# The last pair's products ahead of the first inverse's, in a mixed trunk of gating, RWKV-7 and gated FFN layers

## The chip, the cores and the metric

One Trainium2 chip, one core. The metric is the device time of one execution in microseconds (us). The kernel before takes 1244.08 us, the median of 3 runs (1243.03 to 1244.97). For a measurement of this kernel, 0.2% (2.5 us) is about what can be told from no change.

Engines: TensorE (PE, with PEld for its weight loads), VectorE (DVE), ScalarE (ACT), GpSimd (POOL) and SyncE (SP, which here issues DMAs). L12 is line 12 of the kernel.

## The reference, cut to what matters

Two residual layers on x of 512 positions by 1024 channels, float32: a gMLP layer and an RWKV-7 layer, each followed by a convolutional FFN. The change lies in the RWKV-7 layer:

```python
r = xr @ w_r;  k = xk @ w_k;  v = xv @ w_v
w = -softplus(-(w0 + tanh(xw @ w1) @ w2)) - 0.5
a = sigmoid(a0 + (xa @ a1) @ a2)
g = sigmoid(xg @ g1) @ g2
kk = l2norm_per_head(k * k_k)
k = k * (1 + (a - 1) * k_a)
# per head (16 heads of 64), S is 64 x 64:
#   S_t = S_{t-1} diag(exp(-exp(w_t))) + (S_{t-1} (-kk_t)) (kk_t a_t)^T + v_t k_t^T;  y_t = S_t r_t
y = group_norm(y) * ln_w + ln_b
bonus = sum_per_head(r * k * r_k) * v
out = ((y + bonus) * g) @ w_o
```

The recurrence is not run position by position. The 512 positions are cut into 8 chunks of 64, and in each chunk the steps' influence on each other is solved by the inverse of a 64 x 64 triangular matrix, for every chunk and head.

## The kernel before, in words

Activations lie with channels on the 128 partitions and the 512 positions along the free axis. A weight product is done in three passes on pieces of float32 (high times high, high times low, low times high: L325 to L327), 128 x 128 weights against 512 positions.

The RWKV-7 layer (`rwkv_main`) works on 8 *pairs* of heads (128 channels each), in two groups g of four. Its parts are Python generators, and each `yield` is a step by which they are woven together:

- `pairs` (the main line at first): for pair p the decays (`decay`), the scaled operands (`operands`, all on VectorE but a few copies), and the products (`products`): L973 for each half of the chunks into banks "aux" and "us", the masks L977 on VectorE, three DMAs of the result each (L981), then L988 into `bt` (L991) and its DMA (L992). Three steps a pair; the third one only goes on with the decays of a later pair.
- `invert(g)`: the inverses of a group's chunks. It copies blocks (L1046), transposes them on VectorE (`turn`, L1051), runs 30 dependent steps of elimination on VectorE (L1069, L1070; a yield after every second one), transposes twice more, and then does eight batches of small products on TensorE (L1090, L1093), with ScalarE's copies L1098, L1103 and L1105 between. For g = 1 a `turn` is four instructions of 256 columns, for g = 0 one of 1024. Its steps are 1 (after the first transpose), 15 (elimination), 1 (after the last transpose) and 8 (batches); for g = 1 one more at the start.
- `fill`: work for TensorE that is put between the steps of the others. It is the chain of `projections` (key and value weights; a value takes four steps of six matmuls, 512 positions each), `gates` (the gate's low-rank products, 17 steps) and `project` (the output projection, 12 steps for g = 0, then g = 1). A value m (`value`) is copied into `v` (L854), centred (L868, ScalarE's four copies L873), and then its bonus product L883 is multiplied by v on VectorE (L885) into `rt`, and ScalarE adds the bias ln_b there (L886).
- `scan(g)`: 8 chunks of three steps. L1301 are the chunk's first products; they are copied to `wt` (L1304); L1314 multiplies by the inverse; L1321 and L1326 are the state and the output. `finish` normalizes two chunks' outputs (squares L1342, sums L1347, a power on POOL, L1357, transposes L1363, L1366).

In `gates`, two steps issue idle matmuls (`idle`, L1124: two products into a spare place), and the step behind them issues one more such pair each time it is asked before the first group's last normalization has been traced (`while 0 not in normed`). Then `gate` multiplies `rt` by the gate (L1209) and splits it for the projection.

The order is written out at the end of `rwkv_main`. `weave(main, side, fill, rate, lag, side_rate)` runs main step by step; after every step `rate` fills are due, and `side_rate` steps of the side line. The stages are: pairs 0 to 3 with fill; pairs 4 to 7's first step, with `invert(0)` at the side; the last pair's other two steps; what is left of `invert(0)` in a loop; scan 0 with `invert(1)` at the side; scan 1; and a hand-written end. `tc.issue_after(x)` puts instructions behind x on its engine. From the program's order and a cost model of its own the framework's scheduler fixes the order of each engine's instructions ahead of the run.

PSUM has four tags of two banks each: "mm" for the projections, "aux", "e" and "us".

## Time and profile before

| what | value |
|---|---|
| median of 3 runs | 1244.08 us (1243.03 to 1244.97) |
| the profiled execution | 1245.55 us, its span 1243.7 us |
| granted TensorE clock, mean | 0.996 |
| TensorE busy | 1226.8 us (99%) |
| VectorE, ScalarE, POOL busy | 851.1, 633.1, 81.4 us |
| pairs 4 to 7 and the first inverse | about 649 to 726 us of the span |
| scan 0, scan 1 | about 726 to 784, 784 to 840 us |

The span goes from the first to the last instruction. A row of a group gives line, engine, operation, out<-in, shape and count, then busy time in us and the mean in ns of one, then the idle time of the engine just before and what ended it. A timeline row begins with start and length in us; [2.28 <-DVE rt L885] says that the engine had been idle for 2.28 us and that this instruction released it. A row on one line of the code gives the least, median and greatest ns of one, and first and last start. Under it stand who waited for whom, in us and times.

### The profile page before, as it was taken

What the parts mean: (1) busy time and instruction counts of PE and PEld (TensorE: products, weight loads), DVE (VectorE), ACT (ScalarE), POOL (GpSimd) and SP (SyncE); (2) the same over time, 40 slices, a digit from 0 to 9 for tenths busy, and PEclk for the clock granted to TensorE, in tenths of its full rate; (3) what the DMA queues carried; (4) which work ended last, traced back from release to release, by engine and by line L of the source; (5) the groups of instructions that cost most, each with busy time, mean ns of one, the idle gap of its engine ahead of it and who ended that gap; (6) DMA issues with size and microseconds to landing.
All of it is one profiled execution on the core that took longest, in us unless ns stands there. A gap on an engine that the chain in (4) does not pass through costs nothing.

```text
span 1243.7 us, 19411 instructions
## 1 busy us (share of the span) xinstructions
PE 1226.8 (99%) x7535; PEld 1000.2 (80%) x7535; DVE 851.1 (68%) x1418; ACT 633.1 (51%) x1089; POOL 81.4 (7%) x106
## 2 busy tenths in 40 slices
PE   9999999999999999999999999999999999999997
PEld 6878888888888888877887777778888888888886
DVE  5566578888876454675899698776777777872323
ACT  6544455555554343466787667424544444543232
POOL 1100200000000001000000013222000000000000
PEclk9999999999999999999999899999999999999999
DMA  7232457887556776326888797654223223333332
GB/s 273 94 105 82 132 180 246 246 249 241 192 172 193 220 226 196 109 81 182 220 242 237 188 280 233 219 171 135 85 102 102 90 97 102 97 88 104 97 93 81
DMA packets 125133, 201.65 MB, mean 162 GB/s; under 512 B 39857, under 2 KB 63153, under 8 KB 125041
## 3 DMA queue, kind: packets, MB, share of 16 engines
q10 hardware_dynamic: 38976, 112.87, 29.5%
q1 hardware_dynamic: 86064, 87.54, 22.6%
q8 instruction: 59, 0.97, 0.3%
q14 instruction: 34, 0.27, 0.1%
HBM read 152.93 MB, written 47.45 MB: 161 GB/s over the span
## 4 chain that ended last, share of the span: by engine, by line
PE 91%; DVE 4%; DMA 3%; ACT 1%; issue 0%; SPq 0%; POOL 0%; DVEq 0%; POOLq 0%; ACTq 0%
PE mm L325 9%; PE mm L327 9%; PE mm L326 9%; PE aux L325 6%; PE aux L326 6%; PE aux L327 6%; PE e L325 6%; PE e L326 6%; PE us L325 6%; PE e L327 6%; PE us L327 6%; PE us L326 6%; PE us L1314 1%; PE aux L973 1%; PE aux L988 1%; PE us L1321 1%
## 5 line engine op out<-in xcount | busy, mean ns | idle before, releaser
L237 ACT CAST w<-w 128x512 fp32r<-128x512 f32 x340 | 206.5, 611 | 359.8 <-PE aux L327 92.6
L238 DVE TENSOR_TENSOR w<-w,w 128x512 fp32r<-128x512 f32 x340 | 230.5, 680 | 180.2 <-ACT w L237 179.6
L325 PE MATMUL mm<-mxh,w 128*128 128x512 f32 x408 | 167.9, 412 | 2.7 <-DVE rt L885 2.6
L327 PE MATMUL mm<-mxh,w 128*128 128x512 f32 x408 | 161.1, 395 | 0.0
L326 PE MATMUL mm<-mxl,w 128*128 128x512 f32 x408 | 160.6, 394 | 0.0
L325 PEld LDWEIGHTS mm<-mxh,w 128*128 128x128 f32 x408 | 77.0, 189 | 22.8 <-DVE rt L885 3.3
L327 PEld LDWEIGHTS mm<-mxh,w 128*128 128x128 f32 x408 | 77.0, 189 | 17.1 <-issue 0.8
L326 PEld LDWEIGHTS mm<-mxl,w 128*128 128x128 f32 x408 | 77.1, 189 | 16.2 <-issue 1.7
L575 ACT ACTIVATE cv<-z,par 128x512 f32<-128x512 f32 x88 | 71.7, 817 | 26.5 <-DVE z L573 21.2
L325 PE MATMUL aux<-mxh,w 128*128 128x512 f32 x216 | 84.5, 391 | 0.0
L325 PE MATMUL us<-mxh,w 128*128 128x512 f32 x216 | 84.5, 391 | 0.0
L327 PE MATMUL aux<-mxh,w 128*128 128x512 f32 x216 | 84.2, 390 | 0.0
L326 PE MATMUL aux<-mxl,w 128*128 128x512 f32 x216 | 84.1, 389 | 0.0
L326 PE MATMUL us<-mxl,w 128*128 128x512 f32 x216 | 84.1, 389 | 0.0
L327 PE MATMUL us<-mxh,w 128*128 128x512 f32 x216 | 84.1, 389 | 0.0
L354 POOL TENSOR_TENSOR ss<-ss,sq 128x512 f32<-128x512 f32 x24 | 31.7, 1323 | 761.1 <-ACT sq L352 761.1
L325 PE MATMUL e<-mxh,w 128*128 128x512 f32 x208 | 81.4, 391 | 0.0
L326 PE MATMUL e<-mxl,w 128*128 128x512 f32 x208 | 81.1, 390 | 0.0
L327 PE MATMUL e<-mxh,w 128*128 128x512 f32 x208 | 81.0, 389 | 0.0
L576 DVE SCALAR_TENSOR_TENSOR cv<-z,par,cv 128x512 f32<-128x512 f32 x88 | 66.0, 752 | 19.5 <-ACT cv L575 19.5
L577 DVE SCALAR_TENSOR_TENSOR cv<-z,par,cv 128x512 f32<-128x512 f32 x88 | 66.0, 752 | 2.9
L325 PEld LDWEIGHTS aux<-mxh,w 128*128 128x128 f32 x216 | 40.5, 188 | 9.0 <-issue 0.5
(1113 smaller groups left out, 2555.2 us busy)
## 6 DMA issues: line engine op xcount, KB each, us to landing
w<-in_wup ACTq DMA_DIRECT2D x88, 512.0 KB, 3.7
w<-in_wdn ACTq DMA_DIRECT2D x32, 512.0 KB, 3.7
st<-std SPq DMA_DIRECT2D x15, 640.0 KB, 6.6
w<-wkd ACTq DMA_DIRECT2D x16, 512.0 KB, 5.1
w<-wvd ACTq DMA_DIRECT2D x16, 512.0 KB, 5.1
w<-wod ACTq DMA_DIRECT2D x16, 512.0 KB, 4.2
w<-in_wdn ACTq DMA_DIRECT2D x16, 384.0 KB, 3.3
w<-in_wsu ACTq DMA_DIRECT2D x8, 512.0 KB, 3.7
```

What stands on the lines that cost most here:

```text
L237: nc.scalar.copy(hi[r, :n], src)
L238: (lo_eng or nc.vector).tensor_tensor(lo[r, :n], src, hi[r, :n].bitcast(F32), ALU.subtract)
L325: mm(acc, wh, xh, start=first, stop=False)
L326: mm(acc, wh, xl, start=False, stop=False)
L327: mm(acc, wl, xh, start=False, stop=last)
L354: nc.gpsimd.tensor_tensor(self.ss, self.ss, self.sq, ALU.add)
L575: nc.scalar.activation(c, z[:, 2:], AF.Identity, scale=cw(2, i), bias=self.p("conv_b", l * 44 + i))
L576: nc.vector.scalar_tensor_tensor(c, z[:, 1:T + 1], cw(1, i), c, ALU.mult, ALU.add)
L577: nc.vector.scalar_tensor_tensor(c, z[:, 0:T], cw(0, i), c, ALU.mult, ALU.add)
L973: nc.tensor.matmul(qs[hd][:, c - ch.start, :], bk[H[hd], c, C * hd:C * hd + P], ar[H[hd], c, :], start=True, stop=True)
L988: nc.tensor.matmul(qs[hd][:, c, :], bk[H[hd], c, C * hd:C * hd + P], dg[H[hd], c, :], start=True, stop=True)
L1314: nc.tensor.matmul((us, ux)[hd][H[hd], 1, i, :], ti[g][H[hd], i, c, :], wt[H[hd], i, :], start=True, stop=True)
```

## The change

Seven edits, all in the RWKV-7 layer.

1. The side line in the stage of pairs 4 to 7 gets 1.6 steps of the first inverse for a step of the pairs, not 2.2. The last pair's other steps are woven without the inverse; what is left of it comes in the loop behind them. There a fill is issued at every second step, and `invert(1)` advances, only once the first inverse's last transpose has been issued (`turned`).
2. `turn` is four instructions for g = 0 too.
3. The bonus product takes its bank from "e" once pair 7's operands have been issued, and from "aux" once all pairs are done; "mm" before that.
4. `v` has two buffers.
5. The bias ln_b is no longer added on ScalarE (L886, eight instructions). The gate adds it: L1209 becomes (rt + ln_b) x gate in one VectorE instruction.
6. The copy `wt` of a chunk's first products goes from VectorE to ScalarE.
7. The unused side rate of the last pair's stage goes.

```diff
-RATES = ((1.9, 2), (1.9, 6, 2.2), (0.66, 2, 1.15), (0.72, 2), (1.2, 6, 2.2))
+RATES = ((1.9, 2), (1.9, 6, 1.6), (0.66, 2, 1.15), (0.72, 2), (1.2, 6))
...
-                v = ip.tile([P, T], F32, tag="v", bufs=1, name=self.uid("v"))
+                v = ip.tile([P, T], F32, tag="v", bufs=2, name=self.uid("v"))
...
-            q = bank()
+            q = self.acc("aux" if len(done) == KT else "e" if KT - 1 in used else "mm")
             nc.tensor.matmul(q, wb, rt[g][:, i, :], start=True, stop=True)
             b = rt[g][:, i, :]
             V.tensor_tensor(b, q, v, ALU.mult)
-            S.activation(b, b, AF.Identity, bias=self.p("ln_b", m))
...
             def turn(out, src):
-                for bs in [slice(n, n + 8) for n in range(0, 32, 8)] if g == 1 else [slice(0, 32)]:
+                for bs in [slice(n, n + 8) for n in range(0, 32, 8)]:
                     V.transpose(out[:, bs], src[:, bs])
...
             if g == 0:
                 next(fill)
             turn(y.rearrange("p u t -> p t u"), tt.rearrange("p s t -> p t s"))
+            turned.append(g)
             yield
...
-        gx, tail = [], []
+        gx, tail, turned = [], [], []
...
             o = rt[g][:, i, ts]
-            V.tensor_tensor(o, o, q, ALU.mult)
+            V.scalar_tensor_tensor(o, o, self.p("ln_b", 4 * g + i), q, ALU.add, ALU.mult)
...
                 wt = tile_([P, 4, C], "wt", 4)
-                V.tensor_copy(wt, us[:, 0])
+                S.copy(wt, us[:, 0])
...
         load(0, 0)
         ahead = invert(1)
         next(ahead)
-        self.weave(main, inv, fill, *RATES[4], ktiles=STEPS[1])
-        for _ in inv:
-            next(fill)
-            self.step(ahead, (mybir.EngineType.PE,))
+        self.weave(main, None, fill, *RATES[4], ktiles=STEPS[1])
+        for n, _ in enumerate(inv):
+            if turned and n % 2 == 0:
+                next(fill)
+            if turned:
+                self.step(ahead, (mybir.EngineType.PE,))
         ctx.close()
```

## The prediction

> **What bounds the kernel now.** I read the page first: the head, the engines' shares, and the chain that ended last by engine.

> ```profile
> span 1243.7 us, 19411 instructions
> PE 1226.8 (99%) x7535; PEld 1000.2 (80%) x7535; DVE 851.1 (68%) x1418; ACT 633.1 (51%) x1089; POOL 81.4 (7%) x106
> ...
> PE 91%; DVE 4%; DMA 3%; ACT 1%; issue 0%; SPq 0%; POOL 0%; DVEq 0%; POOLq 0%; ACTq 0%
> ```

> TensorE sets the time; it is idle for 1243.7 - 1226.8 = 16.9 us in all. An edit that moves work can win only idle time, or time at a reduced clock, and loses where it adds either. So I next asked for the engines' busy time in seven stretches around the edited code (columns: length, then PE, PEld, DVE, ACT and POOL busy, granted clock, DMA share, GB/s).

> ```profile
> 656.50:694.70 38.20, 36.62 (x321) 29.43 (x320) 37.38 (x89) 23.38 (x51) 0.72 (x3) 1.00 0.90 243
> 694.71:696.99 2.28, 0.00 (x1) 0.01 (x1) 2.11 (x8) 0.70 (x3) 0.00 (x0) 1.00 0.97 238
> 697.97:704.79 6.82, 6.63 (x50) 5.43 (x50) 3.51 (x2) 4.12 (x8) 0.00 (x0) 0.50 0.24 77
> 704.80:725.80 21.00, 21.00 (x345) 16.50 (x343) 13.61 (x34) 16.49 (x29) 1.27 (x2) 1.00 0.75 203
> 725.80:784.20 58.40, 56.27 (x996) 42.73 (x997) 51.77 (x119) 39.56 (x78) 15.93 (x20) 1.00 0.83 261
> 784.20:840.20 56.00, 55.50 (x770) 42.42 (x766) 39.50 (x87) 19.81 (x44) 15.19 (x16) 1.00 0.57 186
> ```

> Rows 1 to 4 are the last pairs, the first inverse and the run-up to the first scan; row 5 is scan 0, row 6 scan 1. VectorE is full in row 1 (37.38 of 38.20). TensorE stands still for 2.28 us in row 2, and a microsecond later it runs 6.82 us at half the clock, which costs another 6.82 x 0.5 = 3.41 us. From there to the first scan it has no gap. The scans hold 2.13 + 0.50 us of idle. TensorE's timeline, and the groups of the bonus and of the bias, name the stall.

> ```profile
> 696.99 0.50 PE L325 MATMUL mm<-mxh,w 128*128 128x512 f32 x1 [2.28 <-DVE rt L885]
> ...
> L885 DVE TENSOR_TENSOR rt<-mm,v x4: 683/690/692, 670.3 to 709.6; 128x512 f32<-128x512 f32 x4
> ...
>   ACT rt L886: 3.6, 4
> ...
>   PE mm L325: 2.6, 2
> ...
> L886 ACT ACTIVATE rt<-rt,par x8: 711/724/727, 671.1 to 761.2; 128x512 f32<-128x512 f32 x8
> ```

> A value projection needs an "mm" bank which the bonus product holds until VectorE's L885 has read it, and L885 queues behind the inverse's steps. ScalarE's bias L886 waits for L885 too.

> **The change, part by part.** *Banks, v, bias.* The stall stands behind the third value's bonus; pair 7's operands have been traced by then, so that bonus goes to an "e" bank; v gets a second buffer, and eight biases of 0.724 us leave ScalarE. The projection then waits for copies of ScalarE alone, which no longer stand behind L885. I take the whole stall and the half clock away: -2.28 - 3.41 = **-5.69**. Bounds: 0, if another wait takes their place, and -5.69.

> *Order.* The next rows are the chain of waits and TensorE's groups from 697 to 725.7 us.

> ```profile
> 699.72 1.07 PE e L1090 x32
> ...
> 715.23 1.08 ACT bt L991 x2
> 716.32 4.70 DMA btd<-bt
> ...
> 722.68 5.08 DMA cbt<-btd
> ...
> 728.28 0.68 PE us L1314 x16
> ```

> ```profile
> L1090 PE MATMUL e<-ix,ti 32*32 32x32 f32 x128 | 3.0, 203 | 0.2 <-DVE ix L1051 0.2
> L1093 PE MATMUL e<-li,off 32*32 32x32 f32 x128 | 2.6, 192 | 0.0
> L973 PE MATMUL us<-ar,bk 64*128 64x128 f32 x16 | 2.3, 285 | 0.0
> L988 PE MATMUL us<-dg,bk 64*128 64x64 f32 x16 | 1.9, 269 | 0.0
> ```

> Now pair 7's products (L973, L988) stand behind the inverse's first batch, and its DMA out and back in ends at 727.76 (722.68 + 5.08), just before the first scan's products. After the change they come first: 2.3 + 1.9 = 4.2 us of TensorE ahead of L1090, and the pair's seven DMA issues (six L981, one L992) stand on SP's queue some 10 us sooner, ahead of the scan's loads; the two transfers of the chain (4.70 and 5.08) are then over before the batches are. VectorE must then do pair 7's four masks and the three transposes in pieces before the first batch:

> ```profile
> L977 DVE TENSOR_TENSOR lq<-aux,cst 128x512 f32<-128x512 f32 x5 | 3.4, 685 | 0.0
> ...
> L1051 DVE STREAM_TRANSPOSE li<-ix x5: 624/666/2025, 656.6 to 717.5; 128x256 f32<-128x256 f32 x4, 128x1024 f32<-128x1024 f32 x1
> ```

> (L977 is in VectorE's groups from 656.5 to 701.5, L1051 among that line's own.) Four masks are 2.74 us; each transpose costs 4 x 0.666 - 2.025 = 0.64 more. The inverse's input for L1090 moves from 699.7 to about 704. TensorE has more than that to do first: 4.2 us of pair 7 and six value steps that stood behind the first batch. A value step is six matmuls: by the tail's rows below, twelve of them go from 840.17 to 843.02, so one is 1.42 us, and six are 8.5. Cover of 12.7 us against a delay of about 4: the delay costs nothing. Without that cover it would be 4 us.

> *Steps of fill.* Counting yields: pairs 4 to 7 make 9 steps and take floor(9 x 1.9) = 17 fills both ways, but 14 instead of 19 steps of the inverse. The last pair takes 2. Then the loop gives one fill before, four after; the fill inside the inverse and the one of LEAD stay. So **three more value steps** run before scan 0, between the inverse's eight batches, where they take the place of the time won above. Scan 0 (24 yields x 0.66 = 15 fills) and scan 1 (17 fills by the trace) then reach every later step three fills sooner. The gate of the first group needs the last normalization of scan 0, which comes at the fourth yield of scan 1 both ways, with the third fill behind it. Before, no fill had to wait there; after, one has to, and issues a third pair of idle matmuls. The other two of the three are projections that were held for the end, where four fills stand now:

> ```profile
> 792.81 1.06 PE e L1124 x4
> ...
> 840.17 0.50 PE L325 MATMUL mm<-mxh,w 128*128 128x512 f32 x1
> 843.02 0.28 PE L325 MATMUL us<-sg,gwh 128*128 128x256 f32 x1
> 844.93 0.40 PE L325 MATMUL mm<-mxh,w 128*128 128x512 f32 x1
> 846.35 0.60 PE L1363 MATMUL aux<-cst,y 128*128 128x128 f32 x4
> 848.17 0.49 PE L325 MATMUL mm<-mxh,w 128*128 128x512 f32 x1
> ```

> Two fills are at 840.17, one at 844.93, one behind the transposes of 846.35; the last group's projection starts at 848.17, when VectorE's gates have delivered. Two remain, so TensorE does nothing from 844.93 to 848.17 but the transposes. Idle matmuls: **+1.06**. Two fills missing at the end: 2 x 1.42 = **+2.85**; the projection's input comes through the chunk's normalization and the gates, so that stretch doesn't shrink.

> *Bias in the gate.* L1209 becomes a three-operand instruction. Its price lies between today's and that of L1366, which has such a form on the same tile:

> ```profile
> L1209 DVE TENSOR_TENSOR rt<-rt,us x8: 276/280/289, 844.2 to 848.9; 128x128 f32<-128x128 f32 x8
> ...
> L1366 DVE SCALAR_TENSOR_TENSOR rt<-aux,par,rt x32: 328/342/351, 751.7 to 848.6; 128x128 f32<-128x128 f32 x32
> ```

> Eight in the tail's chain: 0 to 8 x 0.062 = 0.50. The first ones lie in front of the projection, the last between its matmuls; I take **+0.3**.

> *First products' copy.* wt goes from VectorE to ScalarE.

> ```profile
> L1304 DVE COPY wt<-us x16: 417/425/427, 727.8 to 835.6; 128x256 f32<-128x256 f32 x16
> ...
>   PE us L1314: 1.0, 2
> ...
> L1301 PE MATMUL us<-vu,st 128*64 128x64 f32 x112 | 4.8, 227 | 0.8 <-issue 0.8
> ```

> ScalarE's nearest copy from PSUM, L991 (512 columns), is 1.08 / 2 = 0.54 us by the chain's row, so the copy itself costs no more than 0.12 extra. What counts is the queue. VectorE is busy 51.77 of 58.40 in scan 0, ScalarE 39.56. Ahead of wt may stand four value copies of 0.366, behind it the y copies and the gate's; who waits for wt is L1314. The second inverse also starts earlier: nine of its steps instead of one come before scan 0, into a stretch where VectorE is busy only 13.61 of 21.00. Bounds: +1.0 (as much waiting on ScalarE as on VectorE again) to -2.6 (all idle of both scans). I take **-1.0**, L1314's own wait.

> *The inverse's batches.* From the first batch to the last copy the first inverse needs ScalarE (its groups from 699 to 725.7 us):

> ```profile
> L1098 ACT COPY ti<-li 32x1024 f32<-32x1024 f32 x4 | 4.2, 1044 | 2.7 <-DVE li L1051 2.6
> L873 ACT COPY vt<-mm 64x256 f32<-64x256 f32 x8 | 2.9, 366 | 0.1
> ...
> L1103 ACT COPY off<-e 32x512 f32<-32x512 f32 x4 | 2.3, 578 | 0.1
> L1105 ACT COPY ti<-e 32x512 f32<-32x512 f32 x4 | 2.3, 577 | 0.4 <-PE e L1093 0.4
> ```

> That is 4.2 + 2.3 + 2.3 = 8.8 us of its own, and 2.9 of value copies. TensorE's cover is 3.0 + 2.6 of batches and five value steps, 7.1: 12.7 us. It is enough if ScalarE takes turns well, but the batches now follow one another without pair 7 between them. Bounds 0 and 12 (23.5 us from 699.7 to the end of L1105 before, less 12.7, rounded up); nearest to the row of ScalarE's sum, 8.8 + 2.9 = 11.7 < 12.7. I take **+1.0**.

> **Sum.** -5.69 + 1.06 + 2.85 + 0.3 - 1.0 + 1.0 = -1.5. The profiled execution took 1245.55 (span 1243.7 and 1.85 around it): 1244.05. The median of the runs, 1244.08, lies 1.47 below that execution, so on its scale **1242.6**.

> **The rivals.** *The clock falls in the tail (14%).* The 2.28 us stall was followed by half clock. The tail's new gap, 848.17 - 844.93 less 0.60 for the transposes, is 2.64 us, longer but cut in two. Then up to 3.41 is lost after 848: 1242.6 + 3.4 = 1246.0, or 1244.3 if the clock stays down half as long, which I take. For it: the stall's row. Against: the transposes between. [...]

> *The scans gain more (22%).* VectorE, relieved of wt and of eight inverse steps, ends every wait in the scans (-2.6 in place of -1.0), and the batches cost nothing (-1.0 again): 1242.6 - 2.6 = 1240.0. For it: VectorE at 89% in scan 0. Against: 2.63 us of idle is all there is.

> *Slower: the first inverse comes last and is waited for (18%).* Place: batches five to eight and L1314 of the first chunk. ScalarE serves value copies and the second inverse's copies in between; if the chain takes 17 us instead of 12.7, TensorE idles 4.3, and after such a gap the clock halves, 3.41 more: 1242.6 - 1.0 + 7.7 = 1249.3. It decides when the chain from first batch to last L1105 exceeds 12.7. For it: 23.5 now. Against: pair 7 sat inside those 23.5.

> *It doesn't do what it says (5%).* The projections still stall, on ScalarE's copies of the "mm" bank: 1242.6 + 5.7 = 1248.3.

> **How the numbers follow.** The forecast has 41%, with its own range 1240.2 to 1245.0. Not to be told from no change is +-2.5 us (0.2%) around 1244.08, so faster means below 1241.6: 13 of the forecast's 41, all 22 of the scans' gain, 1 of the tail's 14: 36%. Slower is above 1246.6: 18 + 5, and 1 of the tail: 24%. The rest, 40%, is the same. The range, 1239.0 to 1249.0, leaves out the better half of the scans' gain (11) and the worse half of the slower rival (9).

> **What would show it.** Right: no gap over 1 us and no reduced clock between 690 and 725; L883 of the third value in an "e" bank; three groups of idle matmuls (L1124) instead of two; scan 0 starting at about the same time, with three value steps fewer in it; a gap of some 2.6 us before the last group's projection, in two pieces; wt on ScalarE and no wait for it above 0.5 us. Wrong: a stall between L1090 and L1105, a new half clock, fills left at the end as before, or TensorE's idle time in the scans at 2.6 us or more.

## The result, and the profile after

The changed kernel takes **1256.69 us** (median of 4 runs, 1255.07 to 1256.82), the kernel before beside it 1244.53 (1243.03 to 1245.04): a ratio of **1.0097, with a 95% interval of 1.0079 to 1.0114**. It is 12 us slower, and 7.7 us above the upper end of the predicted range.

The head of its page, and the chain that ended last by engine. This execution took 1256.66 us.

```profile
span 1254.8 us, 19430 instructions
PE 1231.0 (98%) x7539; PEld 1002.5 (80%) x7539; DVE 847.6 (68%) x1411; ACT 633.1 (50%) x1097; POOL 82.4 (7%) x106
...
PE 88%; DVE 6%; ACT 2%; DMA 2%; issue 1%; SPq 0%; POOL 0%; DVEq 0%; POOLq 0%; ACTq 0%
```

TensorE's idle time grew from 16.9 to 1254.8 - 1231.0 = 23.8 us. The next view has the same stretches as the prediction's table, at the marks where they now lie (length, PE, PEld, DVE, ACT and POOL busy, granted clock, DMA share, GB/s).

```profile
656.50:697.90 41.40, 39.55 (x333) 31.36 (x331) 39.20 (x95) 25.50 (x54) 0.73 (x3) 1.00 0.90 239
697.90:700.50 2.60, 0.14 (x2) 0.10 (x1) 2.38 (x9) 2.38 (x4) 0.00 (x0) 1.00 1.00 281
700.50:731.50 31.00, 30.56 (x416) 23.65 (x416) 26.17 (x63) 20.66 (x39) 1.44 (x3) 1.00 0.90 261
731.50:769.28 37.78, 35.84 (x698) 27.24 (x697) 28.05 (x66) 27.32 (x54) 7.50 (x10) 1.00 0.68 204
769.28:771.39 2.11, 0.00 (x1) 0.01 (x2) 0.71 (x1) 1.72 (x3) 1.41 (x1) 0.89 0.30 67
771.39:791.60 20.21, 20.21 (x267) 15.06 (x267) 11.91 (x24) 9.25 (x21) 6.92 (x9) 0.84 0.67 212
791.60:849.26 57.66, 56.47 (x766) 43.03 (x765) 36.15 (x79) 20.43 (x48) 15.84 (x16) 1.00 0.56 181
849.26:858.20 8.94, 6.19 (x50) 5.21 (x49) 5.77 (x18) 2.85 (x9) 1.63 (x1) 1.00 0.36 118
```

Rows 1 to 3 are the run-up to scan 0, rows 4 to 6 scan 0, row 7 scan 1, row 8 the way to the last projection. Row 2 is a new stall and row 5 another one inside scan 0. Half the clock is granted for 6.83 us from 770.93 on, at the end of row 5 and in row 6, and row 8 has 2.75 us of idle. The two scans (rows 4 to 7) hold 5.2 us of idle, where the prediction named 2.6 us or more as a sign of being wrong. The waits of TensorE from 650 to 870 us name what ended them (us in total, times, longest):

```profile
PE mm L868 <- ACT v L854: 2.5, 1, 2.5
PE mm L325 <- ACT mxh L1213: 2.3, 1, 2.3
PE us L1321 <- issue: 2.1, 1, 2.1
...
PE e L1093 <- issue: 0.4, 1, 0.4
...
PE mm L325 <- DVE rt L885: 0.2, 1, 0.2
```

The wait that the change was to remove (L885, 2.28 us) is down to 0.2. Three others of the same size stand in its place. Put at the marks, against before: scan 0 starts 5.8 us later (725.8 to 731.6), scan 1 7.4 us later (784.2 to 791.6), the last group's projection 10.0 us later, and the span ends 11.1 us later. About 1.4 us of this is there before the edited code begins: the same instructions in the same order run 0.3 us behind up to 588 us, and 1.4 us behind after a gap of 0.91 us there, which the trace of before hasn't. Some of the experiments' traces show it and some don't.

### The profile page after: what moved, and what is told of

Read it like the earlier page. It is cut to its first block, busy times and chain, and to the rows that moved or that the text cites. A ratio compares the mean times of both kernels' runs of the same rounds, so it can differ in the third digit from the quotient of the medians.

```text
span 1254.8 us, 19430 instructions
## 1 busy us (share of the span) xinstructions
PE 1231.0 (98%) x7539; PEld 1002.5 (80%) x7539; DVE 847.6 (68%) x1411; ACT 633.1 (50%) x1097; POOL 82.4 (7%) x106
## 4 chain that ended last, share of the span: by engine, by line
PE 88%; DVE 6%; ACT 2%; DMA 2%; issue 1%; SPq 0%; POOL 0%; DVEq 0%; POOLq 0%; ACTq 0%
PE mm L325 9%; PE mm L326 9%; PE mm L327 9%; PE aux L325 6%; PE aux L327 6%; PE aux L326 6%; PE e L325 6%; PE e L326 6%; PE us L325 6%; PE e L327 6%; PE us L326 6%; PE us L327 6%; DVE pr L1068 1%; DVE li L1069 1%; PE aux L972 1%
## 5 line engine op out<-in xcount | busy, mean ns | idle before, releaser
L325 PE MATMUL mm<-mxh,w 128*128 128x512 f32 x408 | 167.5, 411 | 3.9 <-ACT mxh L1213 2.3
L325 PEld LDWEIGHTS mm<-mxh,w 128*128 128x128 f32 x408 | 76.9, 189 | 23.8 <-ACT mxh L1213 2.5
L325 PE MATMUL aux<-mxh,w 128*128 128x512 f32 x216 | 84.5, 391 | 0.0
L325 PE MATMUL us<-mxh,w 128*128 128x512 f32 x216 | 84.5, 391 | 0.0
L325 PE MATMUL e<-mxh,w 128*128 128x512 f32 x208 | 81.4, 391 | 0.0
L325 PEld LDWEIGHTS aux<-mxh,w 128*128 128x128 f32 x216 | 40.5, 188 | 9.1 <-issue 0.5
```

Of the source, the lines that this page charges most:

```text
L325: mm(acc, wh, xh, start=first, stop=False)
```

## The experiments

Three theories were set against each other. FILL: the value steps taken ahead of scan 0 are missing later. WAITS: TensorE, let past one wait, runs on to the next, and the time stays lost there. WT: the copy on ScalarE is late. From the ninth kernel on there was a fourth, FETCH, which the traces of the first eight suggested: TensorE waits for its own code. In the texts on record e5 and e6 are the kernels 5 and 6.

Each run gives a time and the mean granted clock. A reduced clock is lost time that no wait shows (row 6 above: TensorE busy for 20.21 of 20.21 us at a granted clock of 0.84), so the table has, beside the medians, span x granted clock, the time at full clock (medians over the runs; the clock is given in thousandths, and the half clock behind the last product, which costs nothing, counts in it with 1.5 us in the trace of before and 3.0 in that of the changed kernel, so differences under 1.5 us are not read).

| kernel | median us | ratio to before, 95% interval | at full clock | lost to clock |
|---|---|---|---|---|
| before | 1244.1 to 1244.9 | | 1239.8 to 1240.4 | 2.5 to 3.7 |
| changed | 1256.69 | 1.0097 [1.0079, 1.0114] | 1247.3 | 6.9 |
| 1: wt alone | 1245.67 | 1.0009 [0.9998, 1.0020] | 1240.3 | 3.7 |
| 2: banks, v, bias alone | 1248.66 | 1.0038 [1.0022, 1.0054] | 1240.4 | 6.9 |
| 3: order alone | 1254.82 | 1.0076 [1.0060, 1.0093] | 1248.0 | 5.0 |
| 4: changed, three fills fewer in the loop | 1251.05 | 1.0052 [1.0036, 1.0069] | 1244.1 | 5.0 |
| 5: changed, v's copy first | 1250.22 | 1.0043 [1.0028, 1.0059] | 1244.1 | 3.7 |
| 6: changed, scan 0 with 12 fills | 1250.51 | 1.0041 [1.0022, 1.0059] | 1243.5 | 5.0 |
| 7: bias alone | 1250.27 | 1.0043 [1.0028, 1.0058] | 1240.9 | 8.1 |
| 8: banks and v alone | 1248.38 | 1.0027 [1.0016, 1.0038] | 1240.8 | 6.2 |
| 9: changed, code shifted | 1253.96 | 1.0069 [1.0056, 1.0081] | 1245.8 | 6.3 |
| 10: before, code shifted | 1244.39 | 1.0001 [0.9992, 1.0010] | 1239.6 | 2.5 |
| 11: 5 and 6, bias on ScalarE | 1246.25 | 1.0014 [1.0003, 1.0024] | 1241.1 | 3.7 |
| 12: 5 and 6 | 1245.89 | 1.0011 [1.0003, 1.0020] | 1241.3 | 2.5 |

The table already divides the edits in two. Those on the kernel before that leave the order alone (1, 2, 7, 8) have the same time at full clock as before; 2, 7 and 8 lose by the clock. The new order (3, and the changed kernel) costs 7 us at full clock. The second edit, the transposes in four pieces, has no run of its own.

**1. wt alone.**

```diff
-                V.tensor_copy(wt, us[:, 0])
+                S.copy(wt, us[:, 0])
```

> The kernel before with one edit: the copy wt of a chunk's first products on ScalarE. Three theories of the 12 us. FILL (three fills spent before scan 0 are missing later: a third pair of idle matmuls 1.06, two fills at the end 2.85, half a clock in the tail 1.7): this run stays within 2 us of before. WAITS (the new order puts other instructions in front of what TensorE needs: 2.46 us on ScalarE before the third value's centring, 2.11 and 3.41 of half clock in scan 0): within 2 us of before. WT (the copy waits on ScalarE behind value copies): 4 us or more slower than before, with waits for wt in front of L1314 of over 2 us in all.

1245.67 us: +1.1 by the ratio, and its interval holds no change. The copy is neither the loss nor the gain of 1.0 that was forecast. In the changed kernel the copy itself went from 0.425 to 0.373 us.

**2. Banks, v and bias alone; 8. banks and v alone; 7. bias alone.**

```diff
-                v = ip.tile([P, T], F32, tag="v", bufs=1, name=self.uid("v"))
+                v = ip.tile([P, T], F32, tag="v", bufs=2, name=self.uid("v"))
-            q = bank()
+            q = self.acc("aux" if len(done) == KT else "e" if KT - 1 in used else "mm")
```

```diff
-            S.activation(b, b, AF.Identity, bias=self.p("ln_b", m))
-            V.tensor_tensor(o, o, q, ALU.mult)
+            V.scalar_tensor_tensor(o, o, self.p("ln_b", 4 * g + i), q, ALU.add, ALU.mult)
```

Kernel 8 has the first of these, kernel 7 the second, kernel 2 both.

> The kernel before with the bonus product in other banks, v in two buffers and the bias in the gate; order, transposes and wt as before. This is the prediction's term of -5.69 by itself. If the stall of 2.28 us and the 3.41 of half clock were the bonus bank's: about 1239, no gap over 1 us between 690 and 710. If the value copy on ScalarE is next late: a gap of 1 to 2 us stays and the time is 1242 to 1245. FILL and WAITS both say: not slower than before.

> The kernel before, with the bonus in other banks and two value buffers alone. The prediction's term: the stall of 2.28 and the half clock of 3.41 go, 1244.1 - 5.7 = 1238.4. WAITS: TensorE runs on to the inverse's first batch, which VectorE's copies are not ready for; a gap of about 3 us there and half clock behind it: 1243.5 to 1246.

> The kernel before, with the bias in the gate alone and the eight bias copies on ScalarE (L886) left out. FILL: +0.3, no difference that shows (1243.8 to 1245.0). WAITS: the gate's longer instruction starts the tail's copies later, a gap of about 1 us before the last projection: 1245.0 to 1246.0. Both: the stall before the value projection (2.28) stays, since the bank is still held until L885.

TensorE's waits from 690 to 870 us, in kernel 8, then 2, then 7:

```profile
PE mm L868 <- ACT v L854: 2.1, 1, 2.1
PE e L1093 <- ACT off L1103: 1.1, 1, 1.1
PE e L1090 <- DVE ix L1051: 0.9, 1, 0.9
```

```profile
PE e L1089 <- DVE ix L1050: 3.2, 1, 3.2
PE us L1313 <- DVE wt L1303: 1.6, 1, 1.6
PE mm L325 <- ACT mxh L1212: 1.0, 1, 1.0
```

```profile
PE us L1320 <- ACT vu L1315: 2.3, 1, 2.3
PE mm L325 <- DVE rt L885: 2.3, 1, 2.3
PE us L1313 <- DVE wt L1303: 1.2, 1, 1.2
PE mm L325 <- ACT mxh L1212: 1.0, 1, 1.0
```

In kernels 8 and 2 the 2.28 us before the projection are gone, and TensorE waits about as long a few products later: 2.1 + 0.9 us for v and for the inverse's transpose, or 3.2 us for the transpose alone (L1050 here is L1051 of before). In kernel 8 the copy of v comes late because ScalarE still has the bias L886 ahead of it: L886 starts at 698.62, when VectorE's L885 has released it after 1.55 us of ScalarE's idle time, and the copy at 699.25. So these waits come from VectorE, which the elimination fills here (37.38 of 38.20 us in the kernel before), and the bank only decided which product stood waiting for it. With the bias in the gate the wait of 1.0 us before the last projection appears. Kernel 7 shows a second one, 2.3 us in scan 0: there ScalarE's copy L1315 stands behind four copies L873 (1.50 us), L1097 (1.04) and L1113 (0.72), in an order of ScalarE's queue that before, with the bias in it, hadn't. All three kernels have more gaps over 0.9 us than before, and lose to the clock 6 to 8 us in place of 2.5 to 3.7. None of the forecasts had this: all three medians lie above what FILL and WAITS had said of them (kernel 2 not slower than before, kernel 8 at 1243.5 to 1246, kernel 7 at 1243.8 to 1246.0).

**3. Order alone; 4. the changed kernel with three fills fewer.** Kernel 3 is the kernel before with the new rates, `turned` and the new loop. Kernel 4 is the changed kernel with one fill in the loop, as before, in place of four:

```diff
-            if turned and n % 2 == 0:
+            if turned and n == 2:
```

> The kernel before with the new order alone (rates, loop, the second inverse stepped in the loop). FILL: 4 to 6 us slower than before, the tail's gap over 2 us. WAITS: 10 us or more slower, near 1256, with a gap in front of the third value's centring and one in scan 0. WT: within 2 us of before.

> The changed kernel with one fill in the loop behind the last pair, as before, in place of four. FILL: 1.06 + 2.85 + 1.7 = 5.6 us faster than the changed kernel, about 1251, with two groups of idle matmuls and no gap over 1 us ahead of the last group's projection. WAITS: the gap in front of the third value's centring (2.46) stays; TensorE has three value steps less (4.3 us) between the first inverse's batches, so a new gap there of up to 4 us can take back most of it: 1253 to 1257. WT: as the changed kernel, 1255 or more.

The order alone carries +0.76% of the change's +0.97%: near WAITS's 1256 and far from FILL's 4 to 6 us and WT's 2 us. The waits are only in part where WAITS put them. From 690 to 870 us kernel 3 has, among others,

```profile
PE mm L325 <- ACT mxh L1214: 2.1, 1, 2.1
...
PE mm L325 <- DVE rt L885: 1.6, 1, 1.6
...
PE mm L868 <- ACT v L854: 0.8, 1, 0.8
```

The last two follow each other within 3 us ahead of scan 0, and the first is the gap before the last projection. The copy of v starts at 700.13 in kernel 3, behind the second inverse's copies, and at 697.60 before: it is the order that makes it late. Scan 0 has no wait over 1.3 us in kernel 3, and still takes 58.2 us, with 3.41 us of half clock in it.

In kernel 4, taking the changed kernel's three extra fills out gains 5.6 us. That was FILL's number, but the trace of kernel 4 shows that it isn't clean: two waits of 2.9 and 2.5 us, each followed by 3.41 us of half clock, are in it.

```profile
PE e L1093 <- issue: 2.9, 1, 2.9
PE mm L868 <- ACT v L854: 2.5, 1, 2.5
```

The 2.9 us before L1093 look like the inverse's batches waiting for ScalarE. But the releaser is "issue": TensorE waited for nothing that the profile shows. The ninth kernel bears on what that is.

**5. v's copy first.** In the changed kernel ScalarE reaches the copy of v late. Its timeline there:

```profile
694.39 0.83 ACT L1045 COPY ix<-ti 32x768 f32<-32x768 f32 x1
...
696.78 0.83 ACT L1045 COPY ix<-ti 32x768 f32<-32x768 f32 x1
...
697.63 0.83 ACT L1045 COPY ix<-ti 32x768 f32<-32x768 f32 x1
698.49 0.40 ACT L881 ACTIVATE wb<-cst,par 128x128 f32<-128x128 f32 x1
698.91 0.83 ACT L1045 COPY ix<-ti 32x768 f32<-32x768 f32 x1
699.76 0.59 ACT L854 COPY v<-mm 128x512 f32<-128x512 f32 x1
```

The four L1045 are the first copies of the *second* inverse, which nobody needs yet. TensorE has no work from 697.94 on and starts L868 at 700.40. The experiment puts them behind v:

```diff
                 S.copy(v, a)
+                self.vcopy = self.last(mybir.EngineType.Activation)
                 late = value(m, v)
...
-        next(ahead)
+        with tc.issue_after(self.vcopy):
+            next(ahead)
```

> The changed kernel, with the second inverse's first copies issued behind the value copy on ScalarE. WAITS (the 2.46 us gap before L868 is the value copy behind four inverse copies of 0.83 us, and is lost time): the gap goes, 1256.7 - 2.5 = 1254.2. FILL (the time is lost by value steps taken early, a gap removed only lets TensorE run on to the next wait): 1255.5 to 1257, with a gap over 1 us, or half clock, at another place before scan 0.

1250.22 us, 6.5 less than the changed kernel: 3.2 of it at full clock, 3.2 by the clock. Both theories had less. The wait is gone and hasn't come back ahead of scan 0; its longest waits are now

```profile
PE mm L325 <- ACT mxh L1214: 2.3, 1, 2.3
PE us L1322 <- issue: 1.9, 1, 1.9
```

**6. Scan 0 with 12 fills.**

```diff
-RATES = ((1.9, 2), (1.9, 6, 1.6), (0.66, 2, 1.15), (0.72, 2), (1.2, 6))
+RATES = ((1.9, 2), (1.9, 6, 1.6), (0.54, 2, 1.15), (0.72, 2), (1.2, 6))
```

> The changed kernel, with scan 0's rate .54 in place of .66: 12 fills in place of 15, so scan 1 and the tail get their three fills back. FILL: the third pair of idle matmuls goes (-1.06), two fills stand at the end again (-2.85), half clock in the tail goes (-1.7): 1251.0, if scan 0 still has cover enough with 12 fills. WAITS (the fills of scan 0 cover VectorE, which sets scan 0's time): scan 0 gets gaps for each fill missing, three of 1.42 = 4.3, and the time stays at 1255 to 1257.

1250.51 us, 6.2 less: FILL's 1251.0. The third pair of idle matmuls is gone, and the 2.3 us before the last projection are down to 1.0 with no half clock behind them. Scan 0 did not need the three fills: it takes 55.9 us here, with a wait of 2.0 us for "issue" in it, 58.5 before.

**9. The changed kernel with its code shifted; 10. the kernel before with the same shift.** The wait of 2.1 us in scan 0 falls in the middle of 16 equal products L1321, all of whose inputs are there. The page of the changed kernel has a DMA queue q8 of the kind "instruction", 59 packets of 16 KB in all. TensorE has 7539 products and as many weight loads, 15078 / 59 = 255.6 for a packet. That these packets are its code, one for 256 instructions, is an estimate from these counts, which the shift puts to the test. The DMA queues (packets, MB, share of 16 engines), first q8 over the whole execution, then all from 765.50 to 768.86 us, then from 768.86 to 770.04:

```profile
q8 instruction: 59, 0.97, 0.3%
...
q1 hardware_dynamic: 526, 0.87, 106.1%
...
q1 hardware_dynamic: 110, 0.18, 50.4%
q8 instruction: 1, 0.02, 6.1%
```

In the first stretch q1's transfers take 106.1% of the engines' time and q8 has no packet; its next one lands at 770.02 and TensorE starts again at 771.38, 1.36 us later. Counting TensorE's instructions in the traces (a record or two either way), the first one behind this gap is number 9410 in the changed kernel and in kernels 5 and 6 (gaps of 2.11, 1.91 and 1.98 us; 1.36, 1.40 and 1.40 us behind a packet), and the 2.89 us of kernel 4 end at number 7874, six times 256 earlier, 1.38 us behind a packet. The texts on record call this boundary 9409. Before, it is reached 3.9 us after its packet: there the 256 instructions up to it take 5.8 us, in the changed kernel 3.6.

The test leaves the order of all work as it is and only moves the boundaries, by 128 instructions (7603 products and 7603 weight loads on kernel 9's page, 7539 of each on the changed kernel's), in the warming products that run while the first data come:

```diff
-        for _ in range(9):
-            self.nc.tensor.matmul(a, x[:, 0:P], x, start=True, stop=True)
+        for _ in range(73):
+            self.nc.tensor.matmul(a[:, 0:64], x[:, 0:P], x[:, 0:64], start=True, stop=True)
```

> The changed kernel, with 64 more warming products of 64 columns at the start in place of wide ones: TensorE's code is 128 instructions longer ahead of everything, so every 256th instruction (16 KB of code) is another one; order and work are the same. FETCH (the 2.11 us gap in scan 0 is the wait for a late 16 KB packet of code, at the boundary 9409, and trips the half clock behind it): no such gap at that instruction, 2.1 + 3.4 less, 1251 to 1253, or a shorter gap at another boundary, 1253 to 1255. WAITS (the gap is a wait for data in scan 0): the gap stays at the same matmul, 1256.7.

> The kernel before, with the same 128 instructions at the start. FETCH: its blocks of 256 instructions now end elsewhere in the scans; the fastest stretch of 256 there takes 4.3 to 5.1 us near 774 us, so a packet can come late there: 0 to 1.5 us of gap, 1244 to 1247, or up to 1248 with half clock. WAITS: nothing changes, 1243.5 to 1245.5.

Kernel 9's waits from 690 to 870 us:

```profile
PE mm L868 <- ACT v L854: 2.4, 1, 2.4
PE mm L325 <- ACT mxh L1213: 2.3, 1, 2.3
...
PE e L1093 <- issue: 0.7, 1, 0.7
```

The wait before L1321 is gone, the two waits for v and before the last projection are where they were, and the time is 2.7 us less (1253.96; the two intervals of the ratio overlap a little). Scan 0 goes from 60.1 to 55.8 us. This is FETCH's second case: the 0.7 us before L1093 end at number 7874, 1.63 us behind a packet, and since the code is shifted this is other work than what stands at 7874 in the changed kernel. Kernel 10 is not to be told from before: from 690 to 870 us it has no wait for "issue" over 0.3 us. So FETCH is shown for the wait in scan 0. That it explains kernel 4's is carried by the count and by the 1.38 us, not by a run of its own. Five more short waits for "issue" end at such a number, 1.37 to 1.56 us behind a packet: 0.44 us before L1093 in the changed kernel, 0.46 in kernel 7, 0.74 in kernel 8, 0.73 and 1.01 in kernel 12.

**11 and 12. Both repairs together.** Kernel 12 is the changed kernel with the edits of 5 and 6; kernel 11 also has the bias back on ScalarE.

> The changed kernel with the second inverse's first copies behind the value copy, scan 0's rate at .54, and the bias back on ScalarE (so banks, order, pieces and first products' copy remain of the change). FILL and WAITS together: the 2.46 gap (e5: -3.2 of full-clock time) and the late fills (e6: -3.8) add up to 7.0, and the tail's 0.95 goes: about 1243 to 1246. If they do not add (each only lets TensorE run on to the same next wait): 1248 to 1251.

> As the run before it, but with the bias in the gate as the change has it. Prediction's term: +0.3 against that run. WAITS: the tail's copies start about 1 us later, +1.0, and more half clock if a gap near 2 us appears in the scans as with the bias alone: +1 to +5.

1246.25 and 1245.89 us. The two repairs take 10.8 of the 12.2 us (the two alone 6.5 and 6.2, so they add up but for 1.9). What is left of kernel 12's waits are sums of 1.0 us or less. Among the longest are

```profile
PE e L1327 <- issue: 1.0, 1, 1.0
PE us L1322 <- DVE rb L1316: 1.0, 1, 1.0
PE mm L325 <- ACT mxh L1214: 1.0, 1, 1.0
```

The first of these ends at number 9410. Where the bias stands makes no difference that shows (11 against 12, where +0.3 or +1 to +5 had been forecast), though the 1.0 us before the last projection is in 12 alone: against it 11 waits 1.9 us for v's copy, in spite of kernel 5's edit. Neither kernel beats the one before (1.0014 and 1.0011, both intervals above 1). With the long waits gone, the new order reaches 1241 us at full clock and the old one 1240, so no gain shows behind them.

## Why the prediction was wrong

**The step that failed first is the term -5.69 of "Banks, v, bias".** Both halves of it were no gain.

- *The stall of 2.28.* "The projection then waits for copies of ScalarE alone, which no longer stand behind L885." They did not stand behind L885; v's copy stood behind four copies of the second inverse (3.3 us of ScalarE), which this step did not look for, and TensorE waited 2.46 us for it. Only the rival "it doesn't do what it says" had a stall on ScalarE's copies, at 5%, and there a projection waited for its bank; here the centring L868 waited for v. Where the order was left alone it waited 3.2 us for the elimination (kernel 2) or 2.1 + 0.9 (kernel 8). The step's bound "0, if another wait takes their place" was the right value at full clock; by the clock kernels 8 and 2 are 3.5 and 4.6 us slower than before.
- *The half clock of 3.41.* It was taken from the profiled execution and booked as a property of the stall. Kernel 10 has the same stall, 2.29 us for L885, with no half clock in it. Its two stretches of 3.41 us around the stall, at full clock in spite of 1.10 and 1.54 us of idle (columns as in the first table of stretches):

```profile
693.16:696.57 3.41, 2.31 (x9) 1.23 (x7) 3.25 (x10) 2.28 (x5) 0.00 (x0) 1.00 0.85 197
696.57:699.98 3.41, 1.87 (x8) 1.42 (x8) 3.26 (x7) 1.92 (x3) 0.00 (x0) 1.00 0.80 232
```

In more than half of the runs it seems not to be there at all: 34 of the 61 runs of before beside the experiments have a mean clock of 0.998 or 0.999, like kernel 10's profiled one (0.998), against 0.996 in the profile of before. Setting the sum against the profiled execution and then moving it by -1.47 carried the error over.

The term of the banks and that of the fills (next) were booked at -5.69 + 3.91 = -1.8 together. Undoing both causes gives back 10.8 us (kernel 12 against the changed kernel).

**Steps of fill** was right in its mechanism: three groups of idle matmuls (below), two fills missing at the end, and a gap in two pieces, 0.44 and 2.31 us, ahead of the last projection.

```profile
L1124 PE MATMUL e<-cst x12: 377/379/483, 789.4 to 798.5; 128*128 128x256 f32 x12
```

```profile
855.24 0.63 PE L1363 MATMUL aux<-cst,y 128*128 128x128 f32 x4 [0.44 <-DVE y L1357]
858.17 0.73 PE L325 MATMUL mm<-mxh,w 128*128 128x512 f32 x2 [2.31 <-ACT mxh L1213]
```

It was booked at 1.06 + 2.85 = 3.91. Kernel 6, which puts the fills back, has 3.8 less at full clock. The half clock behind the gap came on top, 3.41 us long, 1.7 us of cost: the rival "the clock falls in the tail", with its 1.7. What the step left out is what the fills did between: "scan 0 starting at about the same time" was wrong (5.8 us later, of which 1.4 were there before the change begins), since the gain that they were to be put into did not exist.

**What no step had is the wait for code in scan 0**: 2.11 us, and 6.83 us of half clock behind it in that execution. Without it (kernel 9) scan 0 is 2.7 us shorter than before, as three value steps fewer let one expect; with it 1.6 longer. It isn't all that scan 0 lost: kernel 3 has no such wait there, and its scan 0 is 0.3 us shorter than before, not 2.7. The prediction counted yields and durations, and not how fast TensorE runs through its instructions.

**Order.** "The delay costs nothing" held: the first batch starts at 715.9, TensorE is full from 700.5 to it, and no wait stands there. The sizes did not hold: the batch's input is ready at 713.7 and not at 704, a delay of 14 us and not of 4, and the work in front of it covered that too.

**Bias in the gate.** The instruction was bounded well: 0.342 to 0.349 us for the eight at the end against 0.276 to 0.289, and 0.062 each had been assumed.

```profile
L1209 DVE SCALAR_TENSOR_TENSOR rt<-rt,par,us x8: 342/344/349, 853.9 to 859.5; 128x128 f32<-128x128 f32 x8
```

The step's +0.3 was too low for the gap that it opens, 0.95 us in kernels 2, 4, 6, 7 and 12, and none over 0.4 there in kernels 8, 10 and 11. That the change of ScalarE's queue by eight missing instructions moves waits elsewhere (kernel 7: +5.3 us) was not thought of at all.

**First products' copy** was booked at -1.0 and is 0 within the interval, though L1314's wait went as forecast (1.0 us in the trace of before, none in that of the changed kernel). **The inverse's batches**, +1.0, cost nothing that shows: from the first batch at 715.9 to the last copy L1105, which starts at 729.8 and takes 0.58, are 14.5 us, more than the 12.7 from which the slower rival was to decide. TensorE waited 0.44 us among them, at number 7874 of its code and not for ScalarE; that the three extra value steps covered the rest fits, but no run takes it apart. That rival forecast a slower outcome, 1249.3, with the wrong place.

*Still open.* Kernels 2, 7 and 8 lose 2.5 to 4.4 us more to the clock than before beside them. Their gaps of 1 to 3 us fit that, but the executions with the lowest clock (0.992 in kernels 2 and 7) have no trace. Why the stretch ahead of the boundary 9409 is run through in 3.6 us in the changed kernel, 5.8 before, was not taken apart: kernel 6 puts back the later positions of the fills and still has the wait.

## What to carry to other kernels

A wait that is removed from the engine that bounds the kernel is worth at most the distance to its next wait: look at who produces what the next products need, on every queue that leads there, before booking the stall as gain. The half clock behind a stall differed from one execution to the next here (6.83 us of it behind 2.28 us in that of before, none behind 2.29 us in kernel 10's): compare the clocks of several runs before it enters a sum. And a TensorE that was 98% busy still stood for 2.11 us in the changed kernel, waiting for nothing that the profile shows, and went on 1.36 us behind a packet of q8: where many narrow products follow each other, check such a gap against the packets of that queue, and count the instructions up to it.

## What the runs showed of the hardware

**Half clock came in stretches of 3.41 or 6.83 us.** From 8 us on to the last product, every stretch of half clock in the fourteen traces has one of these lengths: in that of before one from 697.97 us on, 6.83 us long, in that of the changed kernel one of 6.83 us from 770.93 on and one of 3.41 from 859.67 on. Within a trace they begin a whole number of 3.413 us apart (these last two 26 times that). Each trace was therefore cut into stretches of 3.413 us, counted from where a half clock of its own begins, and TensorE's idle time was summed in each. The changed kernel, and kernel 9, which differ only in the shifted code, have the same stall before L868, 2.46 and 2.45 us. In the changed kernel it falls into two of these stretches with 1.31 and 1.16 us, and the clock stays (columns as in the first table of stretches; after the two shown it is 1.00 again):

```profile
695.83:699.25 3.42, 2.11 (x10) 1.38 (x8) 3.25 (x10) 3.32 (x6) 0.00 (x0) 1.00 0.83 197
699.25:702.66 3.41, 2.26 (x14) 1.94 (x14) 3.17 (x11) 2.12 (x5) 0.00 (x0) 1.00 0.66 207
```

In kernel 9 2.24 us fall into one stretch, and the next has half the clock:

```profile
696.44:699.85 3.41, 1.17 (x6) 0.61 (x4) 3.13 (x11) 3.31 (x5) 0.00 (x0) 1.00 0.83 223
699.85:703.26 3.41, 3.20 (x12) 2.92 (x13) 3.17 (x9) 1.22 (x4) 0.00 (x0) 0.50 0.35 114
```

**Code.** In four kernels TensorE waited for 1.9 to 2.9 us at number 9410 or 7874 of its instructions, six times 256 apart, and went on 1.36 to 1.40 us after a 16 KB packet of q8 had landed; six shorter waits of 0.4 to 1.0 us ended 1.37 to 1.63 us after one. Most of the numbers that lie a multiple of 256 from 9410 have no wait: in the trace of the changed kernel two of 59 do (0.44 us at 7874, 2.11 us at 9410), in that of before none. Up to 9410 the 256 instructions took 3.6 us in the changed kernel, with q1's transfers at 106.1% of the DMA engines' time from 765.50 to 768.86 us, and 5.8 us before, where the packet had landed 3.9 us earlier.
